# Experts' weights: two row tiles of each matrix multiplied in float32 unsplit, loads of whole rows; the differential heads' low keys doubled

## The chip, the cores and the metric

The kernel runs on one core of a Trainium2 chip. The metric is the device time of one execution in microseconds (us), from the timed runs of the kernel; a profile of one more execution is what the rows below are from. PE is TensorE, ACT is ScalarE, DVE is VectorE, POOL is GpSimd, and SP is SyncE, whose queue issues nearly all DMAs.

## The reference

The model is three layers on 1024 tokens of 1024 numbers, all in float32: a layer with four differential-attention heads beside eight sparse-attention heads, a layer of latent attention, and a block with a Fourier mix, windowed attention and a mixture of 16 experts. The change touches the first layer's differential heads and the experts:

```python
s = einsum('bqhmd,bkhmd->bhmqk', q_blk, k) * scale      # 4 heads, m = 2 maps, d = 64
p = softmax(where(chunk_mask, s + bias, -inf))
p = p[:, :, 0] - lam * p[:, :, 1]
return einsum('bhqk,bkhe->bqhe', p, v)

aff = softmax(h @ w_router)
g, idx = top_k(aff.T, 128)                              # 128 tokens for each of 16 experts
xin = h[idx]
y = (silu(xin @ w_gate) * (xin @ w_up)) @ w_down        # three 1024 x 1024 matrices an expert
out = zeros.at[idx].add(y * g)
```

## The kernel before

**Split products.** A float32 product is made of three multiplications in PE's float32r form. `K.split` writes a matrix as hi (a cast by ACT, line 134) plus lo (the rest, a subtraction by DVE, line 135), and `K.mm3` (lines 139 to 141) multiplies hi by hi, hi by lo and lo by hi into one accumulator. A plain float32 multiplication is used for transposes and a few small products.

**Differential heads** (lines 619 to 695, in `layer0`). Four heads one after another, for each two maps m, for each five packs of query blocks. `load_stack` brings the queries of a map as 128 rows, 64 of hi and 64 of lo (in the other order for m = 1); `kd` holds the hi keys twice, on rows 0 to 63 and 64 to 127; `kl` holds the lo keys of both maps, 64 rows each. A score is two multiplications (line 288): all 128 rows of q with kd, then the 64 hi rows of q with the 64 rows of kl. Between them run other units at fixed places: `gate_units` (weights of the gate, product, tanh by ACT into a tile `gth` at line 772, DVE at 773, a store by SP at 774), and `mod.run`, the adaLN rows: loads of w_ada into a tile `adw` with two buffers (SP, line 1284), scaled and added by POOL (lines 1286 to 1292). `kd`, `kl` and the queries have two buffers each, so that a head's are loaded during the head before. Outside the experts the order of the instructions on each engine and on SP is set by a planner that works with estimated times.

**Experts** (lines 1633 to 1829, in `moe`). Their order is the written one (`manual_schedule`). The weights come in 192 loads of 1 MB, each a quarter matrix of 512 rows by 512 columns in a buffer of four row tiles (`mraw`, `xraw`: 16 buffers). Each quarter is split in two pieces of two row tiles into a ring of four (`ring`, lines 1655 to 1657): the cast by ACT, the subtraction by DVE, or by POOL for one piece in four. `product` multiplies the expert's 128 tokens with eight pieces of a matrix, each 2 x 3 multiplications of 512 columns; before each piece it issues the split of the piece that is four ahead, and a load into a buffer when both of its pieces are split. Between pieces stand the steps of the expert: one-hot rows and the gather of the next expert's tokens (`gather`, an indirect DMA by POOL, line 1748), their transposes and splits (`transposed`), silu and the hidden product (lines 1807 to 1812), the scaled output (1820), and, in the next expert's first product, the scatter (an indirect DMA by POOL that adds, line 1823).

Of the kernel before, what the change touches and what calls it, by code (L numbers as in the profile page):

```python
# [59 lines left out]
WO2_AT = ((4, 0), (5, 0), (6, 0), (7, 0))  # L60
HALF2_AT = [(h, i) for h in range(4, 8) for i in range(4)]

RING, MORE_RAWS, SPARE = 4, 8, 4

ONCE = ("bsb", "bsf", "bsk", "bsk2", "gks", "l2", "lamb", "lamc", "lamx", "le", "p2row", "p2r2", "p2r3", "sl", "vmx", "vss1",
        "tkg1", "tklo", "tkv2", "tkv3", "tkvm")
# [401 lines left out]
def layer0(kk, ps, a, hT, mix_d, gate_d, wo, mod):  # L468
# [136 lines left out]
    with kk.pool(name="b0", bufs=1) as bp:  # L605
        bias_d, rows = bias_rows(kk, ps, a["rel_bias"], a["c_oh1"], 12, 256, 32, "b0", 8.0)
        rows.run(None, bp)
    lamc = lambda_cols(kk, ps, lp, a)
    units.run()
    px.close()  # L610

# [4 lines left out]
    pp = sx.enter_context(kk.pool(name="atp", bufs=2))  # L616
    ax = ExitStack()
    ap_ = ax.enter_context(kk.pool(name="at0", bufs=2))
    gates = gate_units(kk, ps, gx.enter_context(kk.pool(name="gx0", bufs=1)), W, GATE0, hT, gate_d)
    for h in range(4):  # L620
        qk = []
        vh = ap_.tile([P, NT, 2, P], F16, tag="v", name=kk.nm("vh"))
        nc.sync.dma_start(vh, v_d[:, :, :, h * P:(h + 1) * P])
        for m in range(2):
            r0 = P * h + 64 * m
            q = load_stack(kk, ap_, stk_d["qa"], r0, f"qd{m}", lo_first=m == 1)
            kd = ap_.tile([P, S], F32R, tag=f"kd{m}", name=kk.nm("kd"))
# [20 lines left out]
        for i, pack in enumerate(PACK0):  # L648
            parts = offsets(pack)
            n, w = parts[-1][2], len(parts)  # L650
            st = kk.sm([P, 2, 2], tag="dst")
            es = []
            for m in range(2):
                q, kd = qk[m]
                r0 = 64 * m

                def pairs(qb):
                    sl = slice(qb * P, (qb + 1) * P)
# [96 lines left out]
    return q, bias  # L755


def gate_units(kk, ps, pool, W, c0, hT, gate_d):

    nc = kk.nc  # L760
    u = Filler()
# [2 lines left out]
    def unit(c, half):  # L764
# [6 lines left out]
        th = pool.tile([P, 512], F32, tag="gth", name=kk.nm("gth"), bufs=2)  # L771
# [17 lines left out]
    nc.vector.tensor_tensor(o, pv, r2[:, :, None].to_broadcast([P, NT, 64]), op=ALU.mult)  # L789


def lambda_cols(kk, ps, lp, a):

    nc = kk.nc
    lq = lp.tile([1, 256], F32, name="lq")
    for i, nme in enumerate(("e_lam_q1", "e_lam_k1", "e_lam_q2", "e_lam_k2")):
        nc.sync.dma_start(lq[:, 64 * i:64 * i + 64], a[nme])
    l2 = kk.sm([1, 2], tag="l2")
    for i in range(2):
        jl = lp.tile([1, 64], F32, name=kk.nm("jl"))  # L800
# [32 lines left out]
    nc.gpsimd.dma_start(dst[1][row0:row0 + m, :], hl.lo[0:m].bitcast(F32))  # L833


def load_stack(kk, pool, src, row0, tag, lo_first=False, into=None, cols=slice(0, S)):

    t = pool.tile([P, cols.stop - cols.start], F32R, tag=tag, name=kk.nm(tag), bufs=2) if into is None else into
    for z in range(2):
        kk.nc.sync.dma_start(t[64 * z:64 * z + 64, :].bitcast(F32), src[z ^ int(lo_first)][row0:row0 + 64, cols])  # L840
    return t


# [775 lines left out]
def moe(kk, ctx, ax, a, con, aff, h2_d, acc_d, mod_d, raws, after):  # L1619
# [9 lines left out]
    def psum(cols, name):  # L1629
# [7 lines left out]
    quarters = {"w_gate_2": ((0, 0), (0, 1), (1, 0), (1, 1)), "w_up_2": ((0, 0), (0, 1), (1, 0), (1, 1)),  # L1637
                "w_down_2": ((0, 0), (1, 0), (0, 1), (1, 1))}
    pairs = [a[w][e][512 * k:512 * k + 512, 512 * n:512 * n + 512] for e in range(NE) for w, q in quarters.items() for n, k in q]
    count = {"load": 0, "split": 0, "use": 0}  # L1640

    def load_ahead(n):
        while count["load"] < min(n, len(pairs)):
            i = count["load"]
            src = pairs[i].rearrange("(k p) n -> p k n", p=P)
            with kk.tc.issue_after(after[min(i, len(after) - 1)]) if i < len(first) else ExitStack():
                for z in ((0, 4),) if i + 1 < len(pairs) else ((0, 2), (2, 4)):
                    nc.sync.dma_start(raws[i % len(raws)][:, z[0]:z[1]], src[:, z[0]:z[1]])
            count["load"] += 1

    def split_ahead(n, spare=False):
        while count["split"] < min(n, 2 * len(pairs)):
            i = count["split"]
            raw, w = raws[i // 2 % len(raws)][:, i % 2 * 2:i % 2 * 2 + 2], ring[i % RING]
            nc.scalar.copy(w.hi, raw)  # L1655
            eng = nc.gpsimd if spare or i % SPARE == 0 else nc.vector
            eng.tensor_tensor(w.lo, raw, w.hi.bitcast(F32), op=ALU.subtract)  # L1657
            count["split"] += 1
            load_ahead(len(raws) + count["split"] // 2)

    load_ahead(len(raws))
    with kk.tc.issue_after(con["last"]):
        split_ahead(RING, True)

# [74 lines left out]
    def gather(e):  # L1739
# [11 lines left out]
        nc.vector.tensor_tensor(gate, gate, sel[:, 4:5], op=ALU.add)  # L1751
        return idx, gate, x, cp

    def transposed(x, xT, g):

        pt = ps.tile([P, 4, P], F32, name=kk.nm("ptx"), **ptag)
        for j in range(4):
            nc.tensor.transpose(pt[:, j, :], x[:, (4 * g + j) * P:(4 * g + j + 1) * P], kk.ident)
        kk.split(xT[:, 4 * g:4 * g + 4, :], pt)

    def product(xT, w, between, done):

        acc = {}
        for q, (n, k4) in enumerate(quarters[w]):
            if k4 == 0:
                acc[n] = ps.tile([P, 512], F32, tag=f"{w}{n}", name=kk.nm(w), bufs=1)
            for h in range(2):
                if 2 * q + h in between:
                    between[2 * q + h]()
                split_ahead(count["use"] + RING)  # L1770
                piece = ring[count["use"] % RING]
                count["use"] += 1
                for j in range(2):
                    k = 4 * k4 + 2 * h + j
                    kk.mm3(acc[n], xT[:, k, :], piece[:, j], k == 0, k == NK - 1)
            if k4:
                done(n, acc[n])

    ctx.enter_context(kk.tc.manual_schedule())
# [10 lines left out]
    def x_part(e, g):  # L1790
        if e < NE:
            if g == 0:
                xT[e] = HL(xp, [P, NK, P], kk.nm("xT"), tag="xT", bufs=1)
            transposed(sel[e][2], xT[e], g)

    step_one_hots(0)
# [3 lines left out]
    step_one_hots(1)  # L1800
    for e in range(NE):
        act = xp.tile([P, D], F32, tag="mth", name=kk.nm("mth"), bufs=1)
        hT = HL(xp, [P, NK, P], kk.nm("hT"), tag="hTm", bufs=1)

        def silu(n, pa):
            h = act[:, 512 * n:512 * n + 512]
# [20 lines left out]
def tile_model(ctx: ExitStack, tc: tile.TileContext, a: dict, out: bass.AP, part=None):  # L1827
# [110 lines left out]
    raws = [rp.tile([P, 4, 512], F32, name=f"mraw{i}") for i in range(8)]  # L1938
    h2s = [raws[i][:, 2 * z:2 * z + 2].rearrange("p k n -> p (k n)") for i in (6, 7) for z in range(2)]
# [187 lines left out]
```

## Time and profile before

| | |
|---|---|
| timed runs, median | 2709.04 us (2708.21 to 2719.33, 3 runs) |
| profiled execution | 2720.05 us, of which span of the trace 2718.2 us |
| PE busy | 2389.0 us (88%) |
| DVE busy | 1957.9 us (72%) |
| ACT busy | 1362.6 us (50%) |
| POOL busy | 786.6 us (29%) |
| data moved | 525.92 MB, mean 193 GB/s |

PE's busy time is the union of its records; since multiplications are pipelined and a record lasts past the start of the next one, their pace is read from start to start. A wait is put down to the instruction or DMA that ended last before it. In a timeline the number in brackets is the engine's idle time before the row and what ended it. PEclk is the granted share of PE's full clock.

### The profile page before, as it was taken

The page shows a single profiled execution, that of the slowest core. Times are in us where ns is not written, and L with a number is a line of the kernel's source. Part 1 is how long each engine was busy: PE and PEld are TensorE (multiplying, and loading weights), DVE is VectorE, ACT ScalarE, POOL GpSimd, SP SyncE. Part 2 cuts the span into 40 slices and gives each one's busy share as a digit, 9 for nine tenths or more (in the row PEclk, how much of TensorE's full clock was granted, in tenths as well). Part 3 has the DMA queues.
Part 4 walks back from the last instruction along what each step waited for, and adds up shares of the span by engine and source line. Part 5 has one row for each costly group of instructions (what it writes and reads, how often), then busy time and mean ns, then how long its engine had stood idle before and what let it go on. Part 6 is the DMA issues. An engine that isn't in the chain of part 4 may idle for free.

```text
span 2718.2 us, 41502 instructions
## 1 busy us (share of the span) xinstructions
PE 2389.0 (88%) x14604; PEld 1913.7 (70%) x14604; DVE 1957.9 (72%) x4594; ACT 1362.6 (50%) x2487; POOL 786.6 (29%) x755
## 2 busy tenths in 40 slices
PE   7988988988978978999889889999849888898988
PEld 6866755756767966787677669887737666676766
DVE  4459978888757354567766677686768788878877
ACT  4344564565534333455644343464326566666655
POOL 0000037577740012000000220110324554545544
PEclk9999988988989999999999989799869899999989
DMA  4433275846655157655754625455769999999992
GB/s 125 135 114 113 109 196 161 214 141 194 184 177 174 46 176 281 177 151 143 212 146 127 214 71 144 114 144 172 277 228 323 307 312 317 312 312 318 310 309 62
DMA packets 347104, 525.92 MB, mean 193 GB/s; under 512 B 43894, under 2 KB 187406, under 8 KB 346896
## 3 DMA queue, kind: packets, MB, share of 16 engines
q1 hardware_dynamic: 330768, 465.59, 54.7%
q0 software_dynamic: 16128, 57.68, 6.5%
q8 instruction: 115, 1.88, 0.3%
q14 instruction: 93, 0.76, 0.1%
HBM read 407.27 MB, written 115.65 MB: 192 GB/s over the span
## 4 chain that ended last, share of the span: by engine, by line
PE 56%; DMA 14%; DVE 12%; POOL 8%; issue 6%; ACT 3%; SPq 1%; POOLq 0%; DVEq 0%; ACTq 0%
PE sb L139 6%; PE sb L140 6%; PE sb L141 6%; PE sb L288 5%; DMA adw<-w_ada 4%; DVE tkj L392 3%; PE ptp L335 3%; PE w_gate L140 2%; POOL ring_l L1657 2%; PE w_gate L141 2%; PE w_down L140 2%; PE w_gate L139 2%; PE w_down L139 2%; PE w_down L141 2%; PE w_up L140 2%
## 5 line engine op out<-in xcount | busy, mean ns | idle before, releaser
L1657 DVE TENSOR_TENSOR ring_l<-mraw,ring_h 128x1024 fp32r<-128x1024 f32 x141 | 223.0, 1602 | 55.4 <-ACT ring_h L1655 54.9
L1657 DVE TENSOR_TENSOR ring_l<-xraw,ring_h 128x1024 fp32r<-128x1024 f32 x144 | 225.5, 1587 | 51.1 <-ACT ring_h L1655 50.4
L1655 ACT CAST ring_h<-xraw 128x1024 fp32r<-128x1024 f32 x192 | 198.8, 1050 | 89.8 <-issue 47.0
L1655 ACT CAST ring_h<-mraw 128x1024 fp32r<-128x1024 f32 x192 | 198.3, 1049 | 88.5 <-issue 43.5
L336 ACT CAST pTh<-ptp 128x512 f16<-128x512 f32 (+2 forms) x316 | 167.0, 555 | 141.1 <-PE ptp L335 132.7
L337 DVE TENSOR_TENSOR pTl<-ptp,pTh 128x512 f16<-128x512 f32 (+2 forms) x316 | 199.6, 648 | 45.7 <-ACT pTh L336 45.2
L1657 POOL TENSOR_TENSOR ring_l<-mraw,ring_h 128x1024 fp32r<-128x1024 f32 x51 | 152.1, 2985 | 145.0 <-ACT ring_h L1655 145.0
L335 PE MATMUL ptp<-ident,e 128*128 128x128 f32 x1184 | 185.7, 288 | 3.9 <-ACT e L1235 1.5
L1657 POOL TENSOR_TENSOR ring_l<-xraw,ring_h 128x1024 fp32r<-128x1024 f32 x48 | 145.0, 3021 | 138.5 <-ACT ring_h L1655 138.5
L140 PE MATMUL w_gate<-ring_l,xT_h 128*128 128x512 f32 x256 | 118.9, 464 | 72.6 <-POOL ring_l L1657 63.9
L1902 POOL TENSOR_TENSOR x<-x,gBf 128x1024 f32<-128x1024 f32 x8 | 19.1, 2387 | 465.4 <-DMA x<-xh_d 439.6
L335 PEld LDWEIGHTS ptp<-ident,e 128*128 128x128 f32 x1184 | 136.7, 147 | 17.5 <-issue 5.1
L1286 POOL TENSOR_SCALAR adw<-adw,ada_s 128x256 f32<-128x256 f32 x192 | 109.5, 581 | 102.7 <-DMA adw<-w_ada 102.2
L347 PEld LDWEIGHTS <-pTl 128*128 128x128 f16 x1184 | 109.6, 100 | 35.9 <-issue 15.8
L345 PEld LDWEIGHTS <-pTh 128*128 128x128 f16 x1184 | 111.3, 101 | 33.1 <-issue 24.4
L1235 ACT ACTIVATE e<-e,nmx 128x1024 f32<-128x1024 f32 (+7 forms) x128 | 98.5, 771 | 65.2 <-DVE nmx L1233 64.3
L890 ACT ACTIVATE e<-e,nmx 128x1024 f32<-128x1024 f32 (+7 forms) x128 | 98.6, 772 | 62.4 <-DVE nmx L889 39.3
L140 PEld LDWEIGHTS w_gate<-ring_l,xT_h 128*128 128x128 f32 x256 | 56.9, 222 | 98.1 <-POOL ring_l L1657 70.4
L139 PE MATMUL w_gate<-ring_h,xT_h 128*128 128x512 f32 x256 | 114.7, 448 | 0.0
L346 PEld LDWEIGHTS <-pTh 128*128 128x128 f16 x1184 | 111.3, 100 | 4.5 <-issue 3.6
L141 PE MATMUL w_gate<-ring_h,xT_l 128*128 128x512 f32 x256 | 113.9, 445 | 0.0
L139 PE MATMUL sb<-hold_h,w_h 128*128 128x512 f32 x272 | 108.2, 398 | 1.5 <-DVE tkatkc L389 1.5
(585 smaller groups left out, 7926.8 us busy)
## 6 DMA issues: line engine op xcount, KB each, us to landing
mraw<-w_gate SPq DMA_DIRECT2D x32, 1024.0 KB
mraw<-w_up SPq DMA_DIRECT2D x32, 1024.0 KB
xraw<-w_up SPq DMA_DIRECT2D x32, 1024.0 KB
xraw<-w_down SPq DMA_DIRECT2D x32, 1024.0 KB
xraw<-w_gate SPq DMA_DIRECT2D x32, 1024.0 KB
mraw<-w_down SPq DMA_DIRECT2D x31, 1024.0 KB
adw<-w_ada SPq DMA_DIRECT2D x96, 256.0 KB
xh_d<-hx SPq DMA_DIRECT2D x48, 256.0 KB
```

Source lines behind the costliest of these rows:

```text
L139: mm(out, a.hi, b.hi, start=start, stop=False)
L140: mm(out, a.hi, b.lo, start=False, stop=False)
L141: mm(out, a.lo, b.hi, start=False, stop=stop)
L288: mm(sc, a, b[:, k0:k0 + n], start=i == 0, stop=i == len(pairs) - 1)
L335: nc.tensor.transpose(pt[:, j, :], p[:, (g + j) * P:(g + j + 1) * P], kk.ident)
L336: nc.scalar.copy(hi[:, g:g + w, :], pt[:, :w, :])
L337: nc.vector.tensor_tensor(lo[:, g:g + w, :], pt[:, :w, :], hi[:, g:g + w, :], op=ALU.subtract)
L345: mm(out, hi[:, j, :], v1(off + j), start=j == 0, stop=False)
L346: mm(out, hi[:, j, :], v2(off + j), start=False, stop=False)
L347: mm(out, lo[:, j, :], v1(off + j), start=False, stop=j == nb - 1)
L1655: nc.scalar.copy(w.hi, raw)
L1657: eng.tensor_tensor(w.lo, raw, w.hi.bitcast(F32), op=ALU.subtract)
```

## The change

In `moe` a load is now 256 whole rows (1 MB, two row tiles by 1024 columns) in 15 buffers. The pieces of a matrix keep their size (two row tiles by 512 columns); gate and up go by columns (all rows of the left half, then of the right), down goes by halves of the rows. The first piece of each half (row tiles 0 and 1) isn't split: it is multiplied straight from the load buffer, once for each row tile, with the tokens in plain float32 (`Operand.full`). The other six pieces of a matrix are split as before, the subtraction always by DVE (by POOL only for the first five, before the loop), into a ring of five. A buffer is loaded again when both column halves were read (`reads`). In the differential heads the lo keys of each map are loaded twice, on 128 rows, three buffers for both maps; the queries are always hi before lo, and the second score multiplication takes all 128 rows too. The gate's tile of these heads has one buffer, and the lambda's two small tiles move to a pool that is closed earlier.

```diff
-RING, MORE_RAWS, SPARE = 4, 8, 4
+RING, MORE_RAWS = 5, 7
...
-    lamc = lambda_cols(kk, ps, lp, a)
+        lamc = lambda_cols(kk, ps, lp, bp, a)
...
-    gates = gate_units(kk, ps, gx.enter_context(kk.pool(name="gx0", bufs=1)), W, GATE0, hT, gate_d)
+    gates = gate_units(kk, ps, gx.enter_context(kk.pool(name="gx0", bufs=1)), W, GATE0, hT, gate_d, bufs=1)
...
-            q = load_stack(kk, ap_, stk_d["qa"], r0, f"qd{m}", lo_first=m == 1)
-            kd = ap_.tile([P, S], F32R, tag=f"kd{m}", name=kk.nm("kd"))
-            for z in range(2):
-                nc.sync.dma_start(kd[64 * z:64 * z + 64, :].bitcast(F32), stk_d["ka"][0][r0:r0 + 64, :])
+            q = load_stack(kk, ap_, stk_d["qa"], r0, f"qd{m}")
+            kd = [ap_.tile([P, S], F32R, tag="kl" if i else f"kd{m}", name=kk.nm("kd"), bufs=2 + i) for i in range(2)]
+            for i in range(2):
+                for z in range(2):
+                    nc.sync.dma_start(kd[i][64 * z:64 * z + 64, :].bitcast(F32), stk_d["ka"][i][r0:r0 + 64, :])
             qk.append((q, kd))
-        kl = ap_.tile([P, S], F32R, tag="kl", name=kk.nm("kl"))
-        nc.sync.dma_start(kl.bitcast(F32), stk_d["ka"][1][P * h:P * h + P, :])
...
-                    return (q[:, sl], kd), (q[r0:r0 + 64, sl], kl[r0:r0 + 64])
+                    return [(q[:, qb * P:(qb + 1) * P], k) for k in kd]
...
-    first, raws = raws[:6], raws[:6] + [rp.tile([P, 4, 512], F32, name=f"xraw{i}") for i in range(MORE_RAWS)] + raws[6:]
+    first, raws = raws[:6], raws[:6] + [rp.tile([P, 2, D], F32, name=f"xraw{i}") for i in range(MORE_RAWS)] + raws[6:]
+    by_cols = [(n, k) for n in range(2) for k in range(4)]
+    order = {"w_gate_2": by_cols, "w_up_2": by_cols, "w_down_2": [(n, 2 * h + k) for h in range(2) for n in range(2) for k in range(2)]}
+    loads_ = [a[w][e][256 * k:256 * k + 256, :] for e in range(NE) for w in order for k in range(4)]
+    pieces = [(4 * m + k, n, k) for m in range(3 * NE) for n, k in order[list(order)[m % 3]]]
+    splits = [i for i, (_, _, k) in enumerate(pieces) if k]
+    slot_of = {i: j % RING for j, i in enumerate(splits)}
...
+    def load_ahead():
+        while count["load"] < len(loads_) and (count["load"] < len(raws) or reads[count["load"] - len(raws)] == 2):
             i = count["load"]
...
+            (nc.gpsimd if spare else nc.vector).tensor_tensor(w.lo, raw_of(i), w.hi.bitcast(F32), op=ALU.subtract)
             count["split"] += 1
-            load_ahead(len(raws) + count["split"] // 2)
...
+            read(i)
...
+    class Operand:
...
+            self.full = xp.tile([P, 2, P], F32, tag=tag + "_f", name=kk.nm(tag + "f"), bufs=1)
+            self.hl = HL(xp, [P, NK - 2, P], kk.nm(tag), tag=tag, bufs=1)
...
-        kk.split(xT[:, 4 * g:4 * g + 4, :], pt)
+        if g == 0:
+            kk.split(xT.hl[:, 0:2, :], pt[:, 2:4])
+            nc.scalar.copy(xT.full, pt[:, 0:2])
+        else:
+            kk.split(xT.hl[:, 2:6, :], pt)
...
+            split_ahead(sum(k > 0 for _, _, k in pieces[:i]) + RING)
+            for j in range(2):
+                if k2 == 0:
+                    nc.tensor.matmul(acc[n], xT.full[:, j, :], raw_of(i)[:, j], start=j == 0, stop=False)
+                else:
+                    kk.mm3(acc[n], xT.hl[:, 2 * k2 - 2 + j, :], ring[slot_of[i]][:, j], False, k2 == 3 and j == 1)
+            count["use"] += 1
+            if k2 == 0:
+                read(i)
+            if k2 == 3:
                 done(n, acc[n])
```

## Rows read from the trace of the kernel before

**Rows 1.** The page's first line.

```profile
span 2718.2 us, 41502 instructions
```

**Rows 2.** Chain of waits, expert loop: start us, us, what.

```profile
2108.50 2.56 POOL out L1823
...
2370.70 2.56 POOL out L1823
2373.26 2.38 POOL ring_l L1657
...
2633.24 2.57 POOL out L1823
```

**Rows 3.** Table of PE's waits from 2040 us on: total us, times, longest.

```profile
PE w_gate L140 <- POOL ring_l L1657: 63.9, 15, 4.5
PE w_gate L140 <- DVE ring_l L1657: 8.7, 14, 1.7
PE w_up L140 <- DVE ring_l L1657: 1.7, 1, 1.7
```

**Rows 4.** PE's timeline in one expert: start us, us, instruction.

```profile
2375.69 0.80 PE L140 MATMUL w_gate<-ring_l,xT_h 128*128 128x512 f32 x1 [4.44 <-POOL ring_l L1657]
...
2381.41 0.49 PE L141 MATMUL w_gate<-ring_h,xT_l 128*128 128x512 f32 x1
...
2383.83 0.40 PE L139 MATMUL w_up<-ring_h,xT_h 128*128 128x512 f32 x1
...
2389.89 0.40 PE L141 MATMUL w_up<-ring_h,xT_l 128*128 128x512 f32 x1
```

**Rows 5.** Busy time by stretch: us, each engine's (count), PEclk, DMA share, GB/s.

```profile
2376.00:2381.00 5.00, 5.00 (x13) 3.85 (x13) 0.73 (x1) 1.26 (x2) 1.60 (x1) 0.50 1.03 329
...
480.00:530.00 50.00, 49.88 (x273) 36.03 (x273) 42.20 (x131) 27.46 (x72) 24.45 (x40) 0.93 0.90 233
530.00:580.00 50.00, 49.96 (x303) 35.04 (x302) 37.83 (x135) 26.78 (x70) 36.15 (x54) 1.00 0.43 130
```

**Rows 6.** Chain of waits after 590 us, first and last adw piece.

```profile
596.97 2.82 DMA adw<-w_ada
...
773.42 3.36 DMA adw<-w_ada
```

**Rows 7.** The ring's subtractions from 2150 to 2588: ns min/median/max.

```profile
L1657 DVE TENSOR_TENSOR ring_l<-xraw,ring_h x96: 1207/1218/4128, 2151.0 to 2586.8; 128x1024 fp32r<-128x1024 f32 x96
...
L1657 POOL TENSOR_TENSOR ring_l<-xraw,ring_h x32: 2377/3014/4196, 2154.3 to 2578.7; 128x1024 fp32r<-128x1024 f32 x32
```

**Rows 8.** Plain float32 multiplications: lines 1477, 1301 (ns min/median/max); timeline of 1477.

```profile
L1477 PE MATMUL pcs<-cs,cd x2: 589/641/693, 1706.1 to 1706.7; 64*128 64x512 f32 x2
...
L1301 PE MATMUL pm<-adx,ones x48: 377/377/631, 1229.0 to 1488.9; 128*1 128x256 f32 x48
...
1706.13 1.12 PE L1477 MATMUL pcs<-cs,cd 64*128 64x512 f32 x2
```

**Rows 9.** Busy time by stretch, as rows 5: loads before the loop, the loop.

```profile
1975.00:2000.00 25.00, 4.14 (x15) 3.75 (x16) 18.74 (x41) 3.45 (x4) 9.25 (x4) 0.50 1.05 387
...
2100.00:2600.00 500.00, 440.25 (x1907) 342.36 (x1906) 408.32 (x455) 313.99 (x341) 253.06 (x93) 0.92 0.93 313
```

**Rows 10.** PE's timeline in the differential heads.

```profile
427.02 0.49 PE L288 MATMUL sb<-kl,qd 64*128 64x512 f32 x1
427.44 0.50 PE L288 MATMUL sb<-kd,qd 128*128 128x512 f32 x1
427.88 0.50 PE L288 MATMUL sb<-kl,qd 64*128 64x512 f32 x1
```

**Rows 11.** Gates: timeline of ACT and of SP; a store in the chain of waits.

```profile
451.19 0.60 ACT L772 ACTIVATE gth<-pg 128x512 f32<-128x512 f32 x1
...
453.54 0.42 SPq L774 DMA_DIRECT2D gate_d<-gth  x1
...
377.22 5.50 DMA gate_d<-gth
```

More of the change, by code (lines that the diff above doesn't have):

```diff
@@ L755, in dsa_head, with gate_units @@
     return q, bias
-def gate_units(kk, ps, pool, W, c0, hT, gate_d):
+def gate_units(kk, ps, pool, W, c0, hT, gate_d, bufs=2):
     nc = kk.nc
@@ L770, in unit @@
             kk.mm3(pp, w[c][:, k, :], hT[:, k, sl], k == 0, k == NK - 1)
-        th = pool.tile([P, 512], F32, tag="gth", name=kk.nm("gth"), bufs=2)
+        th = pool.tile([P, 512], F32, tag="gth", name=kk.nm("gth"), bufs=bufs)
         nc.scalar.activation(th, pp, AF.Tanh, scale=0.5)
@@ L789, in norm_o, with lambda_cols @@
     nc.vector.tensor_tensor(o, pv, r2[:, :, None].to_broadcast([P, NT, 64]), op=ALU.mult)
-def lambda_cols(kk, ps, lp, a):
+def lambda_cols(kk, ps, lp, tp, a):
     nc = kk.nc
-    lq = lp.tile([1, 256], F32, name="lq")
+    lq = tp.tile([1, 256], F32, name="lq")
     for i, nme in enumerate(("e_lam_q1", "e_lam_k1", "e_lam_q2", "e_lam_k2")):
@@ L799, in lambda_cols @@
     for i in range(2):
-        jl = lp.tile([1, 64], F32, name=kk.nm("jl"))
+        jl = tp.tile([1, 64], F32, name=kk.nm("jl"))
         nc.vector.tensor_tensor(jl, lq[:, 128 * i:128 * i + 64], lq[:, 128 * i + 64:128 * i + 128], op=ALU.mult)
@@ L833, in proj_store, with load_stack @@
     nc.gpsimd.dma_start(dst[1][row0:row0 + m, :], hl.lo[0:m].bitcast(F32))
-def load_stack(kk, pool, src, row0, tag, lo_first=False, into=None, cols=slice(0, S)):
+def load_stack(kk, pool, src, row0, tag, into=None, cols=slice(0, S)):
     t = pool.tile([P, cols.stop - cols.start], F32R, tag=tag, name=kk.nm(tag), bufs=2) if into is None else into
     for z in range(2):
-        kk.nc.sync.dma_start(t[64 * z:64 * z + 64, :].bitcast(F32), src[z ^ int(lo_first)][row0:row0 + 64, cols])
+        kk.nc.sync.dma_start(t[64 * z:64 * z + 64, :].bitcast(F32), src[z][row0:row0 + 64, cols])
     return t
@@ L1635, in moe @@
     ring = [HL(rp, [P, 2, 512], f"ring{i}") for i in range(RING)]
-    first, raws = raws[:6], raws[:6] + [rp.tile([P, 4, 512], F32, name=f"xraw{i}") for i in range(MORE_RAWS)] + raws[6:]
-    quarters = {"w_gate_2": ((0, 0), (0, 1), (1, 0), (1, 1)), "w_up_2": ((0, 0), (0, 1), (1, 0), (1, 1)),
-                "w_down_2": ((0, 0), (1, 0), (0, 1), (1, 1))}
-    pairs = [a[w][e][512 * k:512 * k + 512, 512 * n:512 * n + 512] for e in range(NE) for w, q in quarters.items() for n, k in q]
+    first, raws = raws[:6], raws[:6] + [rp.tile([P, 2, D], F32, name=f"xraw{i}") for i in range(MORE_RAWS)] + raws[6:]
@@ L1640, in moe @@
     count = {"load": 0, "split": 0, "use": 0}
-    def load_ahead(n):
-        while count["load"] < min(n, len(pairs)):
+    reads = [0] * len(loads_)
+    def load_ahead():
+        while count["load"] < len(loads_) and (count["load"] < len(raws) or reads[count["load"] - len(raws)] == 2):
             i = count["load"]
-            src = pairs[i].rearrange("(k p) n -> p k n", p=P)
+            src = loads_[i].rearrange("(k p) n -> p k n", p=P)
             with kk.tc.issue_after(after[min(i, len(after) - 1)]) if i < len(first) else ExitStack():
-                for z in ((0, 4),) if i + 1 < len(pairs) else ((0, 2), (2, 4)):
+                for z in ((0, 2),) if i + 1 < len(loads_) else ((0, 1), (1, 2)):
@@ L1648, in load_ahead, with raw_of @@
                     nc.sync.dma_start(raws[i % len(raws)][:, z[0]:z[1]], src[:, z[0]:z[1]])
             count["load"] += 1
-    def split_ahead(n, spare=False):
[L1652 to L1657, printed above, removed]
+    def raw_of(i):
+        r, n, _ = pieces[i]
+        return raws[r % len(raws)][:, :, 512 * n:512 * n + 512]
@@ L1658, in split_ahead, with read @@
+    def read(i):
+        reads[pieces[i][0]] += 1
+        load_ahead()
+    def split_ahead(n, spare=False):
+        while count["split"] < min(n, len(splits)):
+            i = splits[count["split"]]
+            w = ring[slot_of[i]]
+            nc.scalar.copy(w.hi, raw_of(i))
+            (nc.gpsimd if spare else nc.vector).tensor_tensor(w.lo, raw_of(i), w.hi.bitcast(F32), op=ALU.subtract)
             count["split"] += 1
-            load_ahead(len(raws) + count["split"] // 2)
-    load_ahead(len(raws))
+            read(i)
@@ L1662, in moe @@
+    load_ahead()
     with kk.tc.issue_after(con["last"]):
@@ L1752, in gather, with __init__ @@
         return idx, gate, x, cp
+    class Operand:
+        def __init__(self, tag):
+            self.full = xp.tile([P, 2, P], F32, tag=tag + "_f", name=kk.nm(tag + "f"), bufs=1)
+            self.hl = HL(xp, [P, NK - 2, P], kk.nm(tag), tag=tag, bufs=1)
     def transposed(x, xT, g):
@@ L1758, in transposed @@
             nc.tensor.transpose(pt[:, j, :], x[:, (4 * g + j) * P:(4 * g + j + 1) * P], kk.ident)
-        kk.split(xT[:, 4 * g:4 * g + 4, :], pt)
+        if g == 0:
[3 more added lines that the diff above has]
+            kk.split(xT.hl[:, 2:6, :], pt)
     def product(xT, w, between, done):
         acc = {}
-        for q, (n, k4) in enumerate(quarters[w]):
-            if k4 == 0:
+        for q, (n, k2) in enumerate(order[w]):
+            if k2 == 0:
                 acc[n] = ps.tile([P, 512], F32, tag=f"{w}{n}", name=kk.nm(w), bufs=1)
[L1767 to L1776, printed above, removed]
+            if q in between:
+                between[q]()
+            i = count["use"]
+            split_ahead(sum(k > 0 for _, _, k in pieces[:i]) + RING)
[5 more added lines that the diff above has]
+            count["use"] += 1
+            if k2 == 0:
+                read(i)
+            if k2 == 3:
                 done(n, acc[n])
@@ L1792, in x_part @@
             if g == 0:
-                xT[e] = HL(xp, [P, NK, P], kk.nm("xT"), tag="xT", bufs=1)
+                xT[e] = Operand("xT")
             transposed(sel[e][2], xT[e], g)
@@ L1802, in moe @@
         act = xp.tile([P, D], F32, tag="mth", name=kk.nm("mth"), bufs=1)
-        hT = HL(xp, [P, NK, P], kk.nm("hT"), tag="hTm", bufs=1)
+        hT = Operand("hTm")
         def silu(n, pa):
@@ L1937, in tile_model @@
     rp = ctx.enter_context(kk.pool(name="mraw", bufs=1, side="right"))
-    raws = [rp.tile([P, 4, 512], F32, name=f"mraw{i}") for i in range(8)]
-    h2s = [raws[i][:, 2 * z:2 * z + 2].rearrange("p k n -> p (k n)") for i in (6, 7) for z in range(2)]
+    raws = [rp.tile([P, 2, D], F32, name=f"mraw{i}") for i in range(8)]
+    h2s = [raws[i][:, z] for i in (6, 7) for z in range(2)]
     ax = ExitStack()
```

2 lines of the change are left out of this document (removed).

## The prediction

> **What bounds the kernel now.** I read the page first, for the span [rows 1] and for where TensorE (PE) is short of its full clock; then the chain of waits in the last quarter, the table of PE's waits there, and PE's own timeline through one expert. The last quarter, from about 2020 us to the end, is the expert loop: 16 experts one after another, some 698 us. It repeats: the scatter of an expert's output is issued by GpSimd at 2108.50 and eleven times more before 2633.24, so twelve periods in 524.7 us, 43.7 us each [rows 2]. Each chain through a scatter runs GpSimd scatter (2.56 us), GpSimd subtract (2.38 us), PE: the one split in four that GpSimd does stands behind the scatter in its queue. The table of waits prices that: PE waits 63.9 us in 15 waits for GpSimd's subtract, 10.4 us for VectorE's (DVE), and for nothing else: no DMA is in it [rows 3]. The timeline shows what follows: after a wait of 4.44 us the multiplications run at the half rate, 13 of them taking 5.72 us from 2375.69 to 2381.41, then at full rate, 26 steps in 6.06 us, 0.233 us each [rows 4]; the granted clock of the two stretches is 0.50 (1.2 GHz) and, by the pace, the full 2.4 GHz [rows 5]. So the loop is PE's, with a stall and a slow stretch in each expert. At 0.233 us the 13 would take 3.03 us; the slow stretch costs 2.7 us.
>
> The other stage that is touched, the differential heads (about 367 to 590 us), is different. PE is busy all the time in the two later heads [rows 5], yet the chain of waits around that stage, after 590 us until about 778, hops between GpSimd's and the DMAs of the adaLN weights (adw), with a first and a last such piece in [rows 6]; the same pieces fill 395 to 465 us. That is a second chain, paced by its own two buffers, beside PE.
>
> **Experts: what goes.** GpSimd has no subtract left in the loop, only the gather and the scatter. The queue behind the scatter is then empty, and PE's wait for it goes: 63.9 us less the 1.7 us that belong to the last expert, 62.2 us in 14 experts of 4.44 us. With it go the 14 slow stretches, 14 x 2.7 = 37.8 us. DVE's waits of 10.4 us fall in the same places, where DVE was held by GpSimd: its split takes 1.22 us at the median and up to 4.1 us, GpSimd's 2.4 to 4.2 [rows 7]. I take them off too. Sum: 110 us.
>
> **What comes.** Of a matrix' eight row tiles, two are multiplied once in float32 instead of three times in split form: 2 tiles x 2 halves x 3 matrices x 16 experts = 192 places. Three split multiplications cost 3 x 0.233 = 0.70 us. A float32 one with 512 columns stands in the trace once, with 64 rows: two records, the second of 0.589 us, both within 1.12 us; one with 128 rows and 256 columns has 0.377 us a record, two records a call [rows 8]. A split one lasts 0.39 us in the timeline where its successor starts after 0.233 [rows 4], a tail of 0.16; the second float32 record less that tail is 0.43 us, two are 0.86 us. That is the value I take, since the 256-column one with all rows has 0.377 - 0.16 = 0.22 a record, the same rate. The other bound is the whole call less one tail, 1.12 - 0.16 = 0.96 us, in which a weight load lies open. I know no reason by which two records could take less than 0.86. Cost: 192 x (0.86 - 0.70) = 31 us; at 0.96 it is 50.
>
> **Why PE stays the bound.** An expert takes 43.7 - 4.44 - 2.7 - 0.7 = 35.9 us of PE without its stalls, and 35.9 + 12 x 0.16 = 37.8 with the change. DVE is busy 408 of 500 us, 35.7 us an expert [rows 9]; it does 18 splits in each case (18 of 24 now, 18 of 18 after), now without being held, so it falls well under that. ACT loses six casts. The data: 313 GB/s x 43.7 us = 13.7 MB an expert, gather and scatter among it. At 387 GB/s, which loads of 2 KB rows held from 1975 to 2000 us, that is 35.4 us [rows 9]. The loads now bring rows of 4 KB instead of 2 KB. So DMA has 2 us left, and 15 of 192 loads are there before the loop starts. If that cover were gone, the loop would run at DMA's pace (a rival, below). Held at nothing: a buffer is given back only when both halves of its rows are read, up to half a matrix later (some 6 us), and there are 15 instead of 16; with 11 left ahead of PE at 2.7 us each this is hidden. Five splits instead of four are made on GpSimd before the loop, up to 4.2 us more, beside the search, where GpSimd has nothing else on the chain. I leave 4 us for new small waits.
>
> Loop: -110 + 31 + 4 = -75 us.
>
> The Trainium skill ("DMA: Bandwidth & Descriptors", Specifications) gives a limit of about 358 GB/s from HBM to a core. By it an expert's 13.7 MB would take 38.3 us, 0.5 more than PE, and the loop some 8 us more. The 387 GB/s of [rows 9] are above it, so I keep PE's price.
>
> **Differential heads.** The second score multiplication had 64 rows, now 128 (the low part of the keys doubled). In the timeline each multiplication that follows a change between 128 and 64 rows starts 0.42 to 0.44 us after the one before, and the next weight load begins only then [rows 10]; between equal ones of the same width it is 0.233 [rows 4]. That is about 0.195 us, twice for each of 4 heads x 2 maps x 12 = 96 places: 37 us of PE. Where do they go? In the later two heads PE has no pause, so up to 18 us shorten them; but the adw chain runs on at its own pace until 778 us and the DSA heads behind wait for GpSimd, so I expect most of it to be given back there. On the other side stand three costs, none of which is in the trace: 12 more loads on SP's queue (2 MB); the low keys have three buffers for two maps, so the next head's second one waits, on SP, until the present head's first map is read, and adw loads, biases and gate stores behind it on SP wait too; and the gate's tile has one buffer instead of two. For that one: the store of one gate was issued only at 453.54, after the next gate's tanh at 451.19, and a store can take 5.5 us to land [rows 11]. With one buffer ACT would stand 5 to 8 us there, and the softmax behind it. By the timeline this meets about five of 16 gates, some 24 us at most, part of it beside other waits. Bounds: from -29 us (the later heads in full, half of the earlier) to +20 (all the waits, no gain). I take -4, near zero, because the chain through adw is the row that both ends meet.
>
> By the Trainium skill ("TensorE: Matmul & The Clock Gate", Part 3, "What overlaps and what doesn't") a weight load overlaps a running multiplication only when the row groups differ. Then 128 after 128 rows would not overlap either, the doubled keys would gain nothing, and the sum would be 4 us higher. By [rows 4, 10] it does.
>
> Moving the lambda's two small tiles into another pool touches a few short DVE operations: nothing.
>
> **Sum.** -75 - 4 = -79 us, rounded -80. The profiled execution took 2720.05 us, of which its span 2718.2; the median of the three timed runs is 2709.04, so the profile is 11 us (0.4%) above it. By the profile's time 2640, by the median 2629 us.
>
> **Rivals.**
> 1. *The differential gain is kept* (PE sets that stage and the adw chain catches up). For: PE is full in [rows 5]. Against: [rows 6]. 25 us more: 2604.
> 2. *DMA becomes the bound.* DMA engines are 0.93 busy in the loop now [rows 9]; if 313 GB/s is what they give beside the engines, the 177 loads left and 16 gathers and scatters, 202 MB, take 646 us from about 2028, and PE ends some 14 us later, at 2688 instead of 2718. 30 us, and 4: 2675. Against: 387 GB/s in [rows 9], and no wait for a load in [rows 3].
> 3. *The stall stays.* If DVE is held by GpSimd's descriptor writing as GpSimd's own split was, the wait only loses that split's 2.38 us: 2.06 + 2.7 us stay in 14 experts, 67 us: 2696. Against: splits of 1.2 us beside a scatter, and the ring has five pieces. This is also the case that the change does not do what it says.
> 4. *Slower: the float32 multiplications run at the half clock.* If the granted clock falls from 2.4 to 1.2 GHz in them as it does after a stall [rows 5], one takes 1.72 us: 192 x (1.72 - 0.70) = 196, less 110, plus 4, less 4: 2795. It decides from 1.27 us a piece on ((110 + 192 x 0.70)/192). Against: PE does not pause in them.
>
> **How the numbers follow.** Forecast 0.67, rival 1 0.11, rival 2 0.07, rival 3 0.07, rival 4 0.06, 0.02 for others. Range: forecast and rival 1 hold 0.78; the upper bound of the float32 price gives 2648, with the +20 of the heads 2672, and rival 2 2675, so 2598 to 2676, which leaves out rivals 3 and 4. Half a per cent, 13.5 us, is about what a measurement of this kernel can tell from no change. Faster by more: forecast, rivals 1 and 2, 0.86; within: most of rival 3, 0.07; slower: 0.07.
>
> **What would show it.** Right: no wait for GpSimd in PE's table from 2040 us on; scatters 37 to 39 us apart; granted clock near 1.0 there; float32 pairs at 0.43 us a record; about 390 GB/s when loads run. Wrong: waits for DMA in front of the first piece of a matrix (rival 2), waits for DVE at the start of an expert (rival 3), a clock of 0.5 in the float32 pieces (rival 4), ACT waiting for gate stores or SP standing at the low keys, with the differential stage longer than now.

## The result and the profile after

The changed kernel takes 2640.36 us (median of 4 runs, 2629.75 to 2644.28) beside 2708.62 us for the kernel before on the same chip: ratio 0.9733 (95% interval 0.971 to 0.9756), 72 us shorter (66 to 79). The forecast was 2629. Its profiled execution took 2629.75 us, the shortest of the four, so differences between stages are read from the traces, and sizes of a few us from the medians of many runs.

The span, and the same two kinds of stretch as in [rows 5] and [rows 9] (us, each engine's busy time with its count, in the order PE, PEld, DVE, ACT, POOL, then PEclk, DMA share, GB/s):

```profile
span 2628.0 us, 40820 instructions
```

```profile
480.00:530.00 50.00, 39.39 (x238) 31.78 (x238) 34.40 (x106) 23.95 (x61) 22.95 (x38) 0.83 1.00 244
530.00:580.00 50.00, 44.44 (x286) 35.43 (x284) 40.49 (x141) 28.43 (x73) 38.14 (x59) 0.97 0.50 158
...
2100.00:2600.00 500.00, 500.00 (x2065) 352.95 (x2064) 382.97 (x517) 289.08 (x347) 53.49 (x26) 1.00 0.95 350
```

In the expert loop PE is busy 500 of 500 us at a clock of 1.00, where it was 440.25 at 0.92 [rows 9]. In the differential heads it goes the other way: PE is busy 39 and 44 of 50 us, where it was full [rows 5]. The table of PE's waits from 2016 us to the end has one row, where [rows 3] had 74 us:

```profile
PE w_gate L1792 <- ACT xTf L1776: 0.5, 1, 0.5
```

GpSimd's timeline in the loop (start, us, instruction, idle time before it) holds only a gather (`xg`) and a scatter (`out`) for each expert. The scatters are 37.6 us apart, against 43.7 in [rows 2], and no subtraction follows them:

```profile
2099.48 2.59 POOL L1845 DMA_INDIRECT out<-my,idx  x1 [0.30 <-issue]
2135.25 1.52 POOL L1756 DMA_INDIRECT xg<-h_d,idx  x1 [33.19 <-DVE gate L1759]
2137.07 2.57 POOL L1845 DMA_INDIRECT out<-my,idx  x1 [0.30 <-issue]
...
2174.66 2.58 POOL L1845 DMA_INDIRECT out<-my,idx  x1 [0.30 <-issue]
```

PE's timeline at the start of a matrix shows the float32 pieces, and the chain of waits shows one of them whole:

```profile
2330.67 0.40 PE L141 MATMUL w_gate<-ring_h,xT_l 128*128 128x512 f32 x1
2330.91 1.88 PE L1792 MATMUL w_up<-xraw,xTf 128*128 128x512 f32 x4
2332.22 0.80 PE L139 MATMUL w_up<-ring_h,xT_h 128*128 128x512 f32 x1
2332.86 0.40 PE L140 MATMUL w_up<-ring_l,xT_h 128*128 128x512 f32 x1
2333.09 0.39 PE L141 MATMUL w_up<-ring_h,xT_l 128*128 128x512 f32 x1
```

```profile
2218.31 1.72 PE w_up L1792 x4
```

The four records are two multiplications. From the start of the piece to the second split multiplication behind it pass 2332.86 - 2330.91 = 1.95 us; less 0.23 for the first split one, 1.72 us for two, 0.86 each. The granted clock stays at 1.00 from 2100 to 2600 us (0.50 in a float32 piece would have been rival 4).

Marked by the first multiplication with w_gate, the loop takes 611.0 us (2016.9 to 2628.0), before 698.1 (2020.1 to 2718.2): 87 us shorter, forecast 75. All before the loop is 3.2 us shorter in these two traces; the experiments show that this is no gain of the heads.

### The profile page after: what moved, and what is told of

The parts are those of the page before. It is cut to its first block, busy times and chain, and to the rows that moved or that the text cites. A ratio compares the mean times of both kernels' runs of the same rounds, so it can differ in the third digit from the quotient of the medians.

```text
span 2628.0 us, 40820 instructions
## 1 busy us (share of the span) xinstructions
PE 2338.4 (89%) x14412; PEld 1844.6 (70%) x14412; DVE 1841.4 (70%) x4592; ACT 1265.6 (48%) x2423; POOL 510.7 (19%) x661
## 4 chain that ended last, share of the span: by engine, by line
PE 56%; DMA 17%; DVE 12%; POOL 5%; issue 5%; ACT 3%; SPq 2%; POOLq 0%; DVEq 0%; ACTq 0%
PE sb L139 6%; PE sb L140 6%; PE sb L141 6%; PE sb L288 4%; DMA adw<-w_ada 4%; PE ptp L335 3%; DVE tkj L392 3%; PE w_gate L1792 2%; POOL adw L1283 2%; PE w_up L1792 2%; PE w_down L1792 2%; PE w_gate L139 2%; PE w_gate L141 2%; PE w_gate L140 2%; PE w_up L139 2%
## 5 line engine op out<-in xcount | busy, mean ns | idle before, releaser
L1665 DVE TENSOR_TENSOR ring_l<-mraw,ring_h 128x1024 fp32r<-128x1024 f32 x147 | 178.1, 1222 | 58.8 <-ACT ring_h L1664 56.6
L1665 DVE TENSOR_TENSOR ring_l<-xraw,ring_h 128x1024 fp32r<-128x1024 f32 x136 | 164.7, 1223 | 49.2 <-ACT ring_h L1664 47.9
L1664 ACT CAST ring_h<-mraw 128x1024 fp32r<-128x1024 f32 x152 | 156.2, 1049 | 70.0 <-PE w_gate L141 33.8
L1664 ACT CAST ring_h<-xraw 128x1024 fp32r<-128x1024 f32 x136 | 140.5, 1049 | 58.7 <-PE w_gate L141 26.6
L335 PEld LDWEIGHTS ptp<-ident,e 128*128 128x128 f32 x1184 | 134.8, 145 | 24.4 <-DVE e L668 8.1
L1756 POOL DMA_INDIRECT xg<-h_d,idx x16 | 23.8, 1485 | 506.3 <-DVE gate L1759 465.3
L140 PE MATMUL sb<-hold_l,w_h 128*128 128x512 f32 x272 | 107.6, 395 | 0.0
L288 PE MATMUL sb<-hold_l,q 128*128 128x512 f32 (+3 forms) x384 | 104.7, 361 | 3.0 <-DMA q<-qr 3.0
L141 PE MATMUL sb<-hold_h,w_l 128*128 128x512 f32 x272 | 107.3, 396 | 0.0
L345 PE MATMUL pv<-vh,pTh 128*128 128x64 f16 (+1 forms) x608 | 85.6, 205 | 18.5 <-ACT oa L676 10.3
L312 DVE CUSTOM_DVE_ANT_0 e<-sb,hide 128x512 f32<-128x512 f32 (+3 forms) x128 | 74.5, 583 | 37.4 <-PE sb L288 22.1
```

Source lines behind the costliest of these rows:

```text
L140: mm(out, a.hi, b.lo, start=False, stop=False)
L141: mm(out, a.lo, b.hi, start=False, stop=stop)
L288: mm(sc, a, b[:, k0:k0 + n], start=i == 0, stop=i == len(pairs) - 1)
L335: nc.tensor.transpose(pt[:, j, :], p[:, (g + j) * P:(g + j + 1) * P], kk.ident)
L345: mm(out, hi[:, j, :], v1(off + j), start=j == 0, stop=False)
L1664: nc.scalar.copy(w.hi, raw_of(i))
```

## The experiments

Ratios are to the kernel before, measured beside it; a ratio is turned into us with its 2711 us. "Period" is the time from scatter to scatter, one expert, in the middle of the loop. The kernel in which half of the float32 work is left out was timed once and stands in its own section below.

| kernel | ratio (95% interval) | us | period, us |
|---|---|---|---|
| whole change | 0.9733 (0.971 to 0.9756) | -72 | 37.6 |
| experts' part alone | 0.9709 (0.9687 to 0.973) | -79 | 37.6 |
| heads' part alone | 1.0035 (1.002 to 1.005) | +9 | 43.7 |
| one edit to before: no split on GpSimd | 0.958 (0.9559 to 0.9602) | -114 | 35.96 |
| whole rows, all pieces split, new heads | 0.9607 (0.9582 to 0.9633) | -107 | 35.64 |
| the same with the old heads | 0.9567 (0.9548 to 0.9586) | -117 | 35.64 |
| the same with doubled keys, two gate tiles | 0.9584 (0.9565 to 0.9602) | -113 | 35.64 |
| before with one gate tile | 1.0001 (0.9984 to 1.0019) | 0 | as before |
| before with doubled keys, two gate tiles | 1.0004 (0.9989 to 1.0019) | +1 | as before |
| a quarter of adaLN, old heads | 0.9922 (0.99 to 0.9945) | -21 | as before |
| a quarter of adaLN, doubled keys, two gate tiles | 0.9842 (0.982 to 0.9864) | -43 | as before |
| a quarter of adaLN, the change's heads | 0.9928 (0.9907 to 0.995) | -20 | as before |

### The two parts alone

The heads' part alone, as in the diff ahead of the prediction:

> The heads' part alone (doubled low keys, gate tile of one buffer), experts as before. Theory: what PE gains by equal rows is given back, because the adaLN chain (adw pieces through GpSimd) sets the end of the first layer: the sparse heads still end at 763 to 766 us, the whole is 0 to 6 us shorter than before (2703 to 2709). Rival: the 37 us of PE are a real gain that the experts' profile hid: 20 to 29 us shorter, 2680 to 2690. Second rival: the gate tile's single buffer costs more than the keys give: up to 10 us longer.

Measured: 2720.61 us, 9 longer than before. The second rival's amount held; its reason, the gate tile, is tried by itself below. PE's gain is there: between 360 and 590 us it is busy 181.87 us instead of 209.32, and six multiplications with the doubled keys start within 1.39 us (422.66 - 421.27), 0.23 each, where each change between 64 and 128 rows took 0.42 to 0.44 [rows 10]. The granted clock is 1.00 in both places (421 to 422 us here, 427 to 428 before), so it is not the clock that differs. PE's timeline in the changed kernel, the six in one row and the next instruction:

```profile
421.27 1.55 PE L288 MATMUL sb<-kd,qd 128*128 128x512 f32 x6
422.66 0.23 PE L345 MATMUL pv<-vh,pTh 128*128 128x128 f16 x1
```

The time saved is lost elsewhere, and the first place to look is ACT's table of waits between 360 and 600 us (total, times, longest); it has this row in the heads' part alone, and none for gate stores in the kernel before:

```profile
ACT gth L769 <- DMA gate_d<-gth: 24.4, 8, 7.8
```

> The experts' part alone, the differential heads as before. Theory: the two parts don't touch each other: loop of 611 us instead of 698, scatters 37.6 us apart, so 85 to 87 us by the profile and 64 to 72 us by the medians (the whole change less its 3 us). Rival: the heads' part is needed for or hurts the rest: more than 8 us away from the whole change less 3.

Measured: 2631.5 us, 79 shorter, with the same loop (611.0 us, period 37.6). The parts add up within their intervals: -79 + 9 = -70, the whole -72. The all-split kernels with the new and the old heads differ by 11 us, so the heads' part costs 7 to 11 us by the ratios of all three pairs, though only in the first is that clear of the intervals.

### Is float32 needed?

All eight row tiles split, the rest of the experts' part kept:

```diff
-    splits = [i for i, (_, _, k) in enumerate(pieces) if k]
+    splits = list(range(len(pieces)))
...
-                if k2 == 0:
-                    nc.tensor.matmul(acc[n], xT.full[:, j, :], raw_of(i)[:, j], start=j == 0, stop=False)
-                else:
-                    kk.mm3(acc[n], xT.hl[:, 2 * k2 - 2 + j, :], ring[slot_of[i]][:, j], False, k2 == 3 and j == 1)
+                kk.mm3(acc[n], xT[:, 2 * k2 + j, :], ring[slot_of[i]][:, j], k2 == 0 and j == 0, k2 == 3 and j == 1)
```

> The changed kernel, but all eight row tiles of a matrix split by ACT and DVE and multiplied three times, none in float32; whole rows, ring of five and no split on GpSimd in the loop as in the change. PE needs 37.5 - 12 x 0.16 = 35.6 us an expert. Theory A (float32 is what unloads DVE): DVE has 24 splits x 1.22 = 29.3 us and 28.8 - 22.0 = 6.8 of others (306.64 us busy in 400, 37.6 an expert, less 18 splits), 36.1 us, over PE's 35.6, so PE waits for DVE at the start of an expert and loses clock: 39 us or more an expert, 20 us or more longer than the whole change. Theory B (taking the split from GpSimd is all): 36.1 to 36.5 us an expert, some 20 us shorter than the whole change. Theory C (the transfers are the bound beside PE): 37.3 to 37.8, the same time as the whole change, with PE waiting for loads.

Measured: 2603.87 us, 36 us shorter than the whole change by the medians. The period is 35.64 us, less than any theory gave: the theory that float32 is needed to unload DVE falls, and so does the one of transfers as the bound. The busy time by stretch:

```profile
2100.00:2500.00 400.00, 400.00 (x1884) 322.28 (x1883) 396.16 (x517) 310.44 (x337) 48.98 (x24) 1.00 1.02 383
```

PE is busy all the time at the full clock, DVE 396 of 400 us: DVE's 24 splits just fit. 37.59 - 35.64 = 1.95 us an expert is what 12 float32 pieces of a row tile cost, 0.16 each; over 16 experts 31 us.

The opposite edit, one to the kernel before, with its quarter loads, its ring of four and no float32:

```diff
-            eng = nc.gpsimd if spare or i % SPARE == 0 else nc.vector
+            eng = nc.gpsimd if spare else nc.vector
```

> The kernel before with one edit: in the loop every split's subtraction is DVE's, none GpSimd's. Quarter loads (rows of 2 KB), ring of four, no float32. With whole rows, a ring of five and the heads' part, the same work was 35.64 us an expert, 383 GB/s, DVE 99% busy. Theory (GpSimd's split was the only brake): PE waits for nothing, 35.6 to 36.2 us an expert, loop some 120 us shorter, 2585 to 2600 by the median. Rival (whole rows are needed): 2 KB rows at a DMA share of 0.93 gave 313 GB/s, so 337 GB/s at most, 40.7 us an expert with PE waiting for loads: 2655 to 2670. Rival (the ring of five is needed): waits for DVE of 1 to 4 us at each expert's start with slow stretches behind: 38 to 41 us an expert.

Measured: 2598.55 us, 114 shorter, from this line alone: the theory held that GpSimd's split was the only brake. PE's table of waits for the loop is empty. The subtractions on DVE (ns min/median/max), first in the changed kernel, then with this one edit:

```profile
L1665 DVE TENSOR_TENSOR ring_l<-mraw,ring_h x116: 1211/1224/1226, 2150.5 to 2587.8; 128x1024 fp32r<-128x1024 f32 x116
```

```profile
L1657 DVE TENSOR_TENSOR ring_l<-xraw,ring_h x145: 1217/1221/1230, 2149.0 to 2579.9; 128x1024 fp32r<-128x1024 f32 x145
```

The longest is 1.23 us, before it was 4.13 [rows 7]. Gathers and scatters by GpSimd are still there, so it was GpSimd's subtraction that held DVE, not its gathers and scatters (the descriptor writing of rival 3). That settles the worry of rival 3.

### Where the transfers end

```diff
                 if k2 == 0:
-                    nc.tensor.matmul(acc[n], xT.full[:, j, :], raw_of(i)[:, j], start=j == 0, stop=False)
+                    if j == 0:
+                        nc.tensor.matmul(acc[n], xT.full[:, j, :], raw_of(i)[:, j], start=True, stop=False)
```

> The changed kernel without the float32 multiplications of row tile 1 of each matrix (96 of 192 left out, so that row tile is missing from the products; it is still loaded). PE needs 37.5 - 6 x 0.86 = 32.4 us an expert, DVE 28.8. If the transfers have no limit there, scatters are 32.4 us apart and the loop is some 80 us shorter; if 387 GB/s is what they give, 13.7 MB take 35.4 us; if the 363 GB/s seen beside a DMA share of 0.98 are the limit, 37.6 us, no shorter than the whole change, and PE waits for loads instead.

Measured: one run, of 2570.76 us, and none of the three as put. The first nine periods are 32.8 us, near PE's 32.4; the next four, from 2359.93 to 2498.72 us, are 34.7 on the mean, and PE has idle time. (The last two periods are shorter in every kernel here.) The stretches of both parts:

```profile
2100.00:2300.00 200.00, 198.73 (x877) 147.25 (x876) 173.51 (x244) 132.61 (x159) 24.50 (x12) 1.00 1.03 396
2400.00:2530.00 130.00, 123.47 (x540) 90.58 (x539) 105.44 (x143) 80.96 (x99) 12.24 (x6) 1.00 1.03 395
```

In the second part ACT's casts wait for loads, 11 us in all, which they do not in the first:

```profile
ACT ring_h L1664 <- DMA xraw<-w_down: 4.6, 3, 3.2
```

PE's own idle time is put down to a result of DVE (6.5 us in 7 waits), but the chain of waits behind it goes through DVE's subtraction and ACT's cast to a load; loads of w_down are 49% of that chain from 2300 to 2530 us. So PE first uses up the 15 buffers of stock, then runs at the pace of the transfers, 396 GB/s: an expert's 13.7 MB take 34.6 us at it. By this estimate, from one run, the transfers would bind at about 34.6 us an expert, 1 us under the fastest of the other versions. The Trainium skill ("DMA: Bandwidth & Descriptors", Specifications) has about 358 GB/s as the limit from HBM to a core; the runs here held 383 and 396.

### Why the heads' part costs time

The gate tile alone, and the keys with two gate tiles:

```diff
-        th = pool.tile([P, 512], F32, tag="gth", name=kk.nm("gth"), bufs=2)
+        th = pool.tile([P, 512], F32, tag="gth", name=kk.nm("gth"), bufs=bufs)
```

where `bufs` is 1 in the differential heads.

> The kernel before with one edit: the differential heads' gate tile has one buffer. The heads' part alone was 9 us longer than before although its equal key rows took 27 us off PE's busy time; ACT stood 24.4 us there for gate stores (nothing before). Theory: the single gate tile is the cost: ACT waits some 20 to 25 us for gate stores, PE for gates, and the kernel is 9 us or more longer than before (by 9 to 20). Rival: the low keys' three buffers and 12 more loads are the cost: then this kernel is within 3 us of before.

Measured: no difference (0.9984 to 1.0019). ACT's wait for gate stores is there, yet costs nothing with the old heads:

```profile
ACT gth L772 <- DMA gate_d<-gth: 14.9, 4, 6.9
```

```diff
-    gates = gate_units(kk, ps, gx.enter_context(kk.pool(name="gx0", bufs=1)), W, GATE0, hT, gate_d, bufs=1)
+    gates = gate_units(kk, ps, gx.enter_context(kk.pool(name="gx0", bufs=1)), W, GATE0, hT, gate_d, parts=2)
...
-            w[c] = kk.load_w(pool, W, [(c0 + P * c, P)], tag="wg")
+            w[c] = kk.load_w(pool, W, [(c0 + P * c, P)], tag="wg", parts=parts)
```

This second diff is against the heads' part alone; without `bufs=1` the gate's tile has two buffers again, and its weights come in two halves.

> The heads' part alone, but with two buffers for the gate's tile (the room comes from loading the gate's weights in two halves of 256 KB instead of one of 512 KB). Theory (gate tile is the cost): ACT's wait for gate stores goes, and with the keys' gain the kernel is 0 to 10 us shorter than before, so 9 to 19 us shorter than the heads' part alone. If the adaLN chain holds the stage whatever PE does: equal to before within 4 us. Rival (the low keys' buffers and loads are the cost): it stays 5 to 12 us longer than before.

Measured: 1.0004. The wait for gate stores is gone and the loss with it, but no gain is left. That fits the case of the adaLN chain that holds the stage whatever PE does. ACT has a new wait, though, for the halves of the gate's weights, which would fit too:

```profile
ACT wg_h L134 <- DMA wgraw<-e_w_in: 25.9, 7, 10.6
```

So neither the keys (with two tiles) nor the single tile cost anything alone; together they cost 9 us. To see the chain itself, it was cut:

```diff
-        for q in range(0, NK, 2):
+        for q in range(0, 2, 2):
             w = ap_.tile([P, 2, H], F32, tag="adw", name=kk.nm("adw"), bufs=bufs)
```

> The kernel before with three quarters of the adaLN weights left out (of four pieces adw in each unit only the first is loaded, scaled and added, so the modulation rows are incomplete). It is the reference for the next two. Theory (the adw chain through GpSimd sets the end of the first layer): the sparse heads end well before 764 us, 10 to 40 us shorter than before as a whole. Rival (the chain only runs beside): within 5 us of before.

> The same three quarters of the adaLN weights left out, with doubled low keys and a gate tile of two buffers. With the whole adaLN work the keys were worth nothing (0 to 1 us) although PE was 27 to 30 us less busy. Theory (the adw chain took the gain back): with the chain cut, 15 to 27 us shorter than the kernel before with the same cut. Rival (softmax on ACT and DVE holds the stage, adw or not): within 5 us of it.

> The same three quarters of the adaLN weights left out, with the heads' part as in the change (doubled low keys, gate tile of one buffer). Theory (the gate's store is late because it stands on SP's queue behind adw loads that wait for GpSimd, 4.2 us on the mean from the gate's end to the store's issue): ACT's wait for gate stores falls from 24.4 us to under 8, and the kernel is within 4 us of the one with two gate tiles and the same cut. Rival (the landing of the store, 4.8 us on the mean, is enough by itself): ACT still waits 15 us or more, and it stays 6 to 12 us longer than that one.

Measured: 21 us shorter than before with the old heads, 43 with doubled keys and two gate tiles, 20 with the change's heads. The first two theories held: with the chain cut the keys give 22 us, most of the 27 us by which PE's busy time fell in the heads' part alone. ACT's wait for the halves of the gate's weights is 32.5 us there, longer than with the whole chain, and the gain comes all the same; so that wait is not what took it. The cut takes the chain's GpSimd work, its loads and their places on SP's queue away together; which of them held the stage is not told apart. The shares of the chain of waits from 360 to 760 us, by line, say the same. Before:

```profile
by line: DMA adw<-w_ada 22.5%; POOL adw L1286 10.2%; issue 6.7%; PE sb L288 6.6%; POOL adw L1290 5.0%; POOL acc L1291 4.6%; DVE e L312 4.0%; DMA bias<-b0scr 3.3%; DMA mask_d<-tke 3.2%; PE pg L139 3.1%; PE pg L141 3.0%; PE pg L140 2.9%; DMA 
```

With a quarter of the adaLN work and the old heads:

```profile
by line: PE sb L288 16.2%; PE ptp L335 10.2%; DMA adw<-w_ada 7.4%; issue 4.8%; PE pg L139 4.3%; PE pg L141 4.0%; PE pg L140 4.0%; PE poh L139 3.8%; PE poh L141 3.8%; PE poh L140 3.7%; PE pv L345 3.3%; PE pv L347 3.3%; PE pv L346 3.0%; POOL 
```

The adw pieces, 22.5% of the chain and the first in it, give way to PE's score multiplications.

The third theory, that the gate's store is late because it stands behind adw loads on SP's queue, did not hold as put: ACT's wait grew from 24.4 to 31.6 us, and the single tile, with the gate's weights in one load, costs 43 - 20 = 23 us, more than either theory gave.

```profile
ACT gth L769 <- DMA gate_d<-gth: 31.6, 6, 11.7
```

The cut did not empty SP's queue, though. Its table of waits has

```profile
SPq L1281 <- POOL acc L1285: 57.4, 15, 6.0
```

so SP still stood at adw loads that wait for GpSimd, and this run does not tell the two causes of the late store apart. The 23 us are about the 22 that the keys give: where PE sets the stage, the single tile takes the whole gain back. Where the adaLN chain sets it, the tile costs 9 us with the doubled keys and nothing with the old ones; why it differs there is not settled.

### The version that comes out ahead

> Whole rows, ring of five, every piece split by ACT and DVE, none in float32, and the differential heads as before. If the parts add up: the all-split loop (-108 with the heads' part) and the heads' part taken out (-9): 2591 to 2598 by the median, some 117 us shorter than before and 45 shorter than the whole change. Rival: the heads' part is neutral in this company: 2604.

Measured: 2591.9 us, ratio 0.9567, 117 us shorter than before and some 45 shorter than the whole change. It keeps the change's whole rows and its ring of five, and drops the float32 pieces and the heads' part.

> Whole rows, ring of five, every piece split by ACT and DVE, with doubled low keys and two gate tiles. If the keys are worth nothing beside the adaLN chain: as with the old heads, 2588 to 2597 by the median. If the faster expert loop has nothing to do with it but the keys gain a little once the gate is free: 2578 to 2588.

Measured: 2597.7 us, ratio 0.9584. The intervals overlap with the one before: no gain of the doubled keys is shown here either. Nor do these runs tell the 2591.9 us from the 2598.55 us of the one edit to the kernel before, whose interval overlaps too (0.9559 to 0.9602).

## Why the prediction was right, and where it was wrong

The time fell in the range and 11 us above the forecast. That it came so close is partly luck: the loop gained 12 us more than forecast and the heads' part lost 11 to 15 more, two misses of opposite sign.

**The stalls that go: 110 us, measured 114.** This is the term that stands best: the edit that does only this shortens the loop from 698.1 to 584.6 us in the trace. The base of 35.9 us of PE an expert is 35.96 there. GpSimd's wait, DVE's waits and the slow stretches all hung on one split in four, as [rows 2 to 4] said.

**The float32 pieces: 31 us, measured 31.** 0.86 us a piece against 0.70, from the second record of [rows 8] less the tail; the bound of 0.96 was not reached. What I did not ask is whether they are needed at all. The step "DVE ... does 18 splits in each case" priced DVE only with the split taken off it. With all 24 at the undisturbed 1.22 us of [rows 7] and the 6.8 us of other work that the trace after shows, DVE needs 36.1 us an expert beside PE's 35.9, 0.2 us more, where the float32 pieces add 1.9 us to PE. With all pieces split DVE was busy for 35.3 of the 35.64 us of a period (396 of 400 us). That sum was not made.

**New waits: 4 us, measured 0.5.** PE's table has that one row. With a ring of four and 16 buffers, in the one edit to the kernel before, it has none, so the runs do not show that the larger ring was needed.

**Not in the sum: 0.32 us an expert.** Whole rows and a ring of five bring 35.96 down to 35.64, 5 us in all. Which of the two does it was not tried apart. Together: -114 + 31 - 5 = -88, the loop's -87 against -75 forecast.

**Differential heads: -4, measured +7 to +11.** The step that failed is the choice of a value between -29 and +20 "near zero". Its first half was right: the adaLN chain takes the gain back (+1 with two gate tiles; 22 us when it is cut). The second half was named and not charged: "some 24 us at most, part of it beside other waits" is near the 24.4 us of ACT's wait that was measured, though in 8 waits and not five. I let it cancel against a gain that I had just said would not arrive. That this wait by itself is the cost is not shown, since the single tile alone costs nothing; it is the pair that costs 7 to 11 us. Of the other two costs, SP's queue stands, in the heads' part alone, at the loads of the keys and queries for no longer than 0.9 us at a time. PE's gain itself was worked out as 37 us, and its busy time fell by 27.

**What is left.** In the traces the loop is 87 us shorter, by the medians the experts' part gives 79 (73 to 85). In the all-split kernel with the old heads and in the one edit to the kernel before, loop and medians agree (118 beside 117, 114 beside 114), so the gap, if it is more than noise, goes with the float32 pieces: by the medians they cost 36 and 40 us, with the new and the old heads, in the loop 31, which the intervals do not exclude. Both traces of kernels with all the pieces are of the shortest run of their kernel, and the loop starts anywhere from 2005 to 2027 us in the eleven traces with the whole adaLN work, so whether these 5 to 9 us lie in the loop of longer runs or ahead of it stays open.

**The rivals.** 1: no gain of the heads is kept. 2: the transfers never set the pace at 37.6 or at 35.64 us; only with half of the float32 work left out, where PE needs less than some 34.6 us, do they. 3: no wait for DVE is left. 4: the clock in the float32 pieces is 1.00.

## What to carry to other kernels

Before adding work to unload an engine, write down what that engine would need without the added work: here moving the helper engine's share to DVE with nothing else gave 114 us, and the float32 pieces, meant to make room for it, cost 31 of them. A helper engine whose slow elementwise work sits behind an indirect DMA in its queue can cost far more than it takes off, here through the wait [rows 3], the clock after the wait [rows 5] and the neighbour that it slows [rows 7]. A gain on an engine counts only on the chain that ends last; do not set the costs of the same edit off against it, and try the parts of an edit apart and together: here neither the keys nor the single tile cost anything alone.

## What the runs showed of the hardware

- Beside GpSimd's subtractions some of DVE's took up to 4.1 us instead of 1.22; beside its gathers and scatters alone the longest took 1.23.
- One core's transfers held 396 GB/s for 200 us, and 395 for another 130.
- A float32 multiplication of 128 rows by 512 columns took 0.86 us at full clock, 3.7 times a split one of 0.233, and the granted clock stayed at 1.00 from 2100 to 2600 us, with 12 of them in each expert.
- Multiplications of 128 rows by 512 columns, each with its own weight load, started 0.23 us apart, where alternating 64 and 128 rows took 0.42 to 0.44, both at a granted clock of 1.00. By the Trainium skill ("TensorE: Matmul & The Clock Gate", Part 3, "What overlaps and what doesn't") a weight load overlaps only where the row groups differ; the trace does not agree.
